# A transposed product in two matmuls instead of three: streaming encoder trunk on one Trainium2 core

## The chip, the cores and the metric

The kernel runs as one launch on one core of a Trainium2 chip. Its time is device time in microseconds. Beside the timed runs there is one profiled execution, whose trace gives each instruction's start and duration on each engine: TensorE (PE, with its weight loads as PEld), VectorE (DVE), ScalarE (ACT), GpSimd (POOL) and SyncE (SP, which only issues DMAs here).

## What is computed

The input x is 256 tokens by 1024 channels, float32. Two layers of three sub-layers each follow one another: FFN, mixer, FFN. Mixer 0 is an S5 state-space block, mixer 1 is gMLP. So the order is FFN, S5, FFN, FFN, gMLP, FFN.

```python
def _swiglu(x, w_in, w_out):                 # D_MODEL 1024, D_FF 2816
    gate, up = jnp.split(x @ w_in, 2, axis=-1)
    return (jax.nn.silu(gate) * up) @ w_out
# FFN sub-layer:   h = layernorm(sqrt(2)*h + 0.5*swiglu(h))
# gMLP sub-layer:  z = gelu(h @ w_in + b_in); u, v = split(z); v = layernorm(v)
#                  s = masked W_s applied over the tokens of a 128-block, per head; h = layernorm(sqrt(2)*h + (u*s) @ w_out)
```

## The kernel before

**Numbers in two parts.** Each float32 operand of a large product is split into hi (rounded to fp32r, TensorE's format here) and lo, the rest. A product takes three matmuls: hi by hi, hi by lo, lo by hi. Weights are split on the chip: `Stream` (lines 42 to 151) loads blocks of 128 x 2048 (1 MB) in a fixed order on SP's queue into three raw buffers, ScalarE casts raw to hi, VectorE subtracts hi from raw to give lo. At most five blocks are split ahead (`N_SPLIT`). Each call of `ws.tick()` splits one more block if a place is free; with `ws.lazy` set (in the FFN chunks) the lo subtraction is issued one tick after its hi.

**Tokens.** `make_xt` transposes the 256 tokens (two parts t of 128) on TensorE and writes them to `xt` as hi (`xth`) and lo (`xtl`), for eight slices k of 128 channels. In memory `xt` is ordered part, hi or lo, k, token, so for one k and hi the two token parts lie apart.

**An FFN** has 11 chunks of 256 hidden columns, gate and up. The first two are computed with tokens as the stationary operand and weights as the moving one (`step_in`, `mm3`, 512 columns). From chunk 2 on (from chunk 1 in the first FFN), `chunk_in` computes them transposed: weights (128 x 128) stationary, tokens moving, 256 columns, through `mm3t` (line 205). A chunk has four groups (m, g): m the half of 128 hidden columns, g = 0 gate and g = 1 up. A group is 8 slices k of three matmuls. Gate and up of one m share a PSUM bank. When both are done, `act_t` does Silu of the gate out of PSUM on ScalarE (line 397), and VectorE multiplies the up half in PSUM by it (line 398). `split_gt`, after the next group, splits the result into hi and lo for the output product (lines 406, 407). After chunk c come two output steps for chunk c - 2 (`step_out`, 12 matmuls of 512 columns each). The last three chunks' output products come in `close`, together with the residual, the LayerNorm, and the transposes of the next sub-layer's tokens.

**u of gMLP.** `step_u` computes one head of u (128 columns) transposed, like a group above: 24 matmuls through `mm3t`, then Gelu out of PSUM on ScalarE (line 558), then a tick. For heads 4 to 7, `spatial` follows at once: four matmuls into a PSUM tile `sps` and, for two heads, two VectorE operations each (lines 580, 581); then `split_g` splits the gated result (lines 587, 588).

**What sets the order.** The kernel is written under a manual schedule: each engine runs its instructions in the order in which the program issues them, first in, first out, and waits only on semaphores for data and for buffers. The pools rotate their buffers. All PSUM tiles that matter here (`ips`, `tps`, `zps`, `sps`) come from one pool of four banks (`mm_p`), in turn; the output sums have four banks of their own.

In S5, `yx` (line 1122) uses the same `xt` storage for its own operand of the gate product.

Of the kernel before, what the change touches and what calls it, by code (L numbers as in the profile page):

```python
# [9 lines left out]
F32 = mybir.dt.float32  # L10
F32R = mybir.dt.float32r
I32 = mybir.dt.int32
AF = mybir.ActivationFunctionType
ALU = mybir.AluOpType
PSUM = bass.MemoryType.PSUM

P = 128
D = 1024
KD = D // P
SEQ = 256  # L20
DFF = 2816
FC = 256
NCH = DFF // FC
# [131 lines left out]
def hybrid(ctx: ExitStack, tc: tile.TileContext, a: dict, out: bass.AP, subs=SUBS):  # L155
    nc = tc.nc
# [4 lines left out]
    xt_p = pool("xt", 1)  # L161
    g_p = pool("g", 2)
# [3 lines left out]
    mm_p = pool("mm", 4, space=PSUM)  # L166
# [7 lines left out]
    nc.gpsimd.memset(mhalf, -0.5)  # L174

    h = [const.tile([P, D], F32, name=f"h{t}") for t in range(2)]
    xt = xt_p.tile([P, 2, 2, KD, P], F32R, name="xt")
    xth, xtl = ([xt[:, t, j] for t in range(2)] for j in range(2))

    ws = Stream(nc, raw_p, split_p)  # L180

# [22 lines left out]

    def mm3t(ps, wh, wl, k, start, stop):

        xh, xl = (xt[:, :, j, k] for j in range(2))
        nc.tensor.matmul(ps, wh, xh, start=start, stop=False)  # L208
        nc.tensor.matmul(ps, wh, xl, start=False, stop=False)  # L209
        nc.tensor.matmul(ps, wl, xh, start=False, stop=stop)  # L210

    def load_ln(li, si, eng):
        g = ln_p.tile([P, D], F32, tag="gam", name="gam")
        b = ln_p.tile([P, D], F32, tag="bet", name="bet")
        eng.dma_start(out=g, in_=a["ln_g"][li, si:si + 1, :].broadcast_to([P, D]))
        eng.dma_start(out=b, in_=a["ln_b"][li, si:si + 1, :].broadcast_to([P, D]))
        return g, b
# [51 lines left out]
    def done(ids):  # L269
        for i in ids:  # L270
            ws.done(i)
# [61 lines left out]
    def ffn(ids, li, si, first, last):  # L333
# [4 lines left out]
        def new_gt(c, m):  # L338
            if (c, m) not in gts:
                gts[c, m] = gt_p.tile([P, 2, SEQ], F32R, tag="gt", name="gt")  # L340
            return gts[c, m]
# [31 lines left out]
        def chunk_in(c):  # L373

            for m in range(2):
                ps = mm_p.tile([P, 2, SEQ], F32, tag="mm", name="ips")
                for g in range(2):
                    for k in range(KD):
                        wh, wl = ws.get(ids["in"][c][k // 4])
                        s = slice(512 * (k % 4) + FC * g + P * m, 512 * (k % 4) + FC * g + P * m + P)  # L380
                        mm3t(ps[:, g], wh[:, s], wl[:, s], k, k == 0, k == KD - 1)
                    if (m, g) == (1, 1):
                        done(ids["in"][c])
                    split_gt()
                    if g:
                        act_t(c, m, ps)
                    if (m, g) == (0, 1):
                        finish_g()
                    if (m, g) == (1, 1) and c == NCH - 1:
                        split_gt()  # L390
                    ws.tick()

        def act_t(c, m, ps):
            sgg = g_p.tile([P, 2, SEQ], F32, tag="sgg", name="sgg")
            sg, g = sgg[:, 0], sgg[:, 1]
            x = new_gt(c, m)
            nc.scalar.activation(sg, ps[:, 0], AF.Silu)  # L397
            nc.vector.tensor_tensor(g, ps[:, 1], sg, op=ALU.mult)  # L398
            later.append((x, g))

        later = []

        def split_gt():
            while later:
                x, g = later.pop()
                nc.scalar.copy(x[:, 0], g)  # L406
                nc.vector.tensor_tensor(x[:, 1], g, x[:, 0].bitcast(F32), op=ALU.subtract)  # L407
# [59 lines left out]
            step_in(1, 1)  # L467
        ws.lazy = True
        for c in range(2, NCH):
            chunk_in(c)  # L470
            if c == NCH - 1:
                gb = load_ln(li, si, nc.gpsimd)
            if c < NCH - 1:
                step_out(c - 2, 0)
                step_out(c - 2, 1)
# [53 lines left out]
    def gmlp(plan, par, pool, li, si, first, last):  # L529
        cols, rows = plan  # L530
        b_v, vg, vb, b_u, b_s, _, w_st = par
        v = [pool.tile([P, D], F32, name=f"v{t}") for t in range(2)]
        u = [pool.tile([P, SEQ], F32, name=f"u{h}") for h in range(HEADS)]
# [16 lines left out]
        def step_u(hd):  # L550

            ids = cols[2 + hd // 4]
            ps = mm_p.tile([P, SEQ], F32, tag="mm", name="zps")
            for k in range(KD):
                wh, wl = ws.get(ids[k // 4])
                s = slice(512 * (k % 4) + P * (hd % 4), 512 * (k % 4) + P * (hd % 4) + P)
                mm3t(ps, wh[:, s], wl[:, s], k, k == 0, k == KD - 1)
            nc.scalar.activation(u[hd], ps, AF.Gelu_apprx_tanh, bias=b_u[:, hd:hd + 1])
            if hd % 4 == 3:
                done(ids)  # L560
            ws.tick()
# [38 lines left out]
        for hd in range(HEADS):  # L600
            step_u(hd)
            if hd >= 4:
                spatial(2 * hd - 8)
                for x in range(2):
                    split_g(2 * hd - 8 + x)
# [408 lines left out]
    def s5(plan, res, qp, li, si, first, last):  # L1014
# [105 lines left out]
            nc.scalar.copy(yx(ct, 0), yc.rearrange("p (t k) -> p t k", t=2))  # L1120

        def yx(ct, j):
            return xt[:, :, j, ct]

        def split_y(ct):
            yc = y[ct // 4][:, ct % 4]
# [50 lines left out]
        later = []  # L1177
# [96 lines left out]
    with tc.manual_schedule():  # L1274
# [9 lines left out]
        for n in range(2):  # L1284
            s = slice(512 * n, 512 * n + 512)
# [7 lines left out]
        for n, (kind, li, si) in enumerate(subs):  # L1293
            first, last = n == 0, n == len(subs) - 1
# [49 lines left out]
```

## Time and profile before

| | us |
|---|---|
| timed runs | 986.35, 982.47, 985.27 (median 985.27) |
| profiled execution | 983.81 |
| its span, first to last instruction | 981.7 |
| TensorE busy | 948.4 (97%), 6988 matmuls |
| VectorE busy | 650.1 (66%) |
| ScalarE busy | 425.9 (43%) |
| moved from HBM | 184.07 MB, 198 GB/s with the writes over the span |

Matmuls are pipelined and their durations overlap, so the pace of TensorE is read from start to start. The granted clock is a share of full speed: 1.00 is 2.4 GHz, 0.50 is 1.2 GHz. In a row, `out<-in` names the tiles and "<-" behind an idle time names what ended it. Line numbers are those of the kernel before.

### The profile page before, as it was taken

The numbers are of one execution on the slowest core, as the hardware profiler recorded it, in microseconds if no ns is written. First come the engines' busy times: TensorE is split into PE (matmuls) and PEld (weight loads), VectorE is DVE, ScalarE is ACT, GpSimd is POOL, SyncE is SP. The second block draws the span as 40 slices with busy tenths as digits, with TensorE's granted clock in tenths as the row PEclk, the third lists the DMA queues.
The fourth block names the chain that finished last, engine by engine and source line by source line (L and its number), as shares of the span: only waits on it lengthen the run. The fifth ranks groups of instructions, "written<-read, shape, count | busy, mean of one in ns | idle before, by whom it ended". The sixth has DMA issues, their size and how long they took to land.

```text
span 981.7 us, 16616 instructions
## 1 busy us (share of the span) xinstructions
PE 948.4 (97%) x6988; PEld 860.6 (88%) x6988; DVE 650.1 (66%) x801; ACT 425.9 (43%) x504; POOL 165.6 (17%) x249
## 2 busy tenths in 40 slices
PE   7997999999999999999999999999999999999996
PEld 5996989978887789999997999999879879999995
DVE  5858999778797955455467644536588766453635
ACT  5554355644335445343423634344345445433430
POOL 1868811001572100000002000000011010000001
PEclk9998999999899999999999999999999999999998
DMA  8874796968645665746466674655447457555521
GB/s 278 224 223 162 265 280 220 289 214 285 221 146 183 189 209 179 237 133 233 152 200 216 211 272 154 204 182 179 164 155 275 129 173 265 163 194 192 168 90 43
DMA packets 133354, 195.10 MB, mean 199 GB/s; under 512 B 7120, under 2 KB 103936, under 8 KB 133280
## 3 DMA queue, kind: packets, MB, share of 16 engines
q1 hardware_dynamic: 128432, 182.34, 56.0%
q0 software_dynamic: 4560, 11.19, 3.9%
q8 instruction: 54, 0.88, 0.4%
q10 hardware_dynamic: 288, 0.52, 0.1%
q14 instruction: 20, 0.16, 0.0%
HBM read 184.07 MB, written 9.96 MB: 198 GB/s over the span
## 4 chain that ended last, share of the span: by engine, by line
PE 66%; DVE 18%; DMA 6%; POOL 3%; issue 3%; ACT 2%; SPq 0%; POOLq 0%; DVEq 0%; ACTq 0%
PE ips L210 11%; PE ips L209 11%; PE ips L208 11%; PE acc L201 7%; PE acc L202 7%; PE acc L203 7%; DVE lo L89 4%; DVE lo L97 4%; PE pps L1075 2%; DVE pq L639 1%; PE ips L203 1%; DMA raw<-in_ffn_w_out 1%; DVE prod L639 1%; ACT hi L96 1%; PE ips L201 1%
## 5 line engine op out<-in xcount | busy, mean ns | idle before, releaser
L210 PE MATMUL ips<-xt,lo 128*128 128x256 f32 x1184 | 335.5, 283 | 2.8 <-DVE lo L89 2.2
L208 PE MATMUL ips<-xt,hi 128*128 128x256 f32 x1184 | 335.4, 283 | 0.0
L209 PE MATMUL ips<-xt,hi 128*128 128x256 f32 x1184 | 335.0, 283 | 0.0
L89 DVE TENSOR_TENSOR lo<-raw,hi 128x2048 fp32r<-128x2048 f32 x107 | 242.9, 2292 | 11.1 <-ACT hi L88 10.7
L210 PEld LDWEIGHTS ips<-xt,lo 128*128 128x128 f32 x1184 | 227.1, 192 | 3.6 <-DVE lo L89 2.8
L208 PEld LDWEIGHTS ips<-xt,hi 128*128 128x128 f32 x1184 | 227.1, 192 | 1.5
L209 PEld LDWEIGHTS ips<-xt,hi 128*128 128x128 f32 x1184 | 227.1, 192 | 1.4
L88 ACT CAST hi<-raw 128x2048 fp32r<-128x2048 f32 x107 | 204.1, 1909 | 47.2 <-PE acc L203 26.6
L202 PE MATMUL acc<-lo,gt 128*128 128x512 f32 x352 | 138.5, 393 | 6.6 <-DVE lo L89 6.6
L398 DVE TENSOR_TENSOR sgg<-ips,sgg 128x256 f32<-128x256 f32 x74 | 31.3, 423 | 163.9 <-ACT sgg L397 163.8
L201 PE MATMUL acc<-hi,gt 128*128 128x512 f32 x352 | 138.7, 394 | 0.6 <-ACT gt L406 0.5
L203 PE MATMUL acc<-hi,gt 128*128 128x512 f32 x352 | 137.8, 391 | 0.0
L397 ACT ACTIVATE sgg<-ips 128x256 f32<-128x256 f32 x74 | 28.3, 383 | 214.2 <-PE ips L210 213.0
L221 POOL TENSOR_SCALAR rstd<-mv 128x1 f32<-128x1 f32 x14 | 10.4, 741 | 636.8 <-DVE mv L247 613.0
L97 DVE TENSOR_TENSOR lo<-raw,hi 128x2048 fp32r<-128x2048 f32 (+2 forms) x52 | 89.6, 1754 | 22.6 <-ACT hi L96 22.4
L202 PEld LDWEIGHTS acc<-lo,gt 128*128 128x128 f32 x352 | 66.7, 189 | 20.0 <-DVE lo L89 7.5
L201 PEld LDWEIGHTS acc<-hi,gt 128*128 128x128 f32 x352 | 66.7, 189 | 14.2 <-ACT gt L406 1.3
L203 PEld LDWEIGHTS acc<-hi,gt 128*128 128x128 f32 x352 | 66.5, 189 | 14.3 <-DVE gt L407 0.3
L96 ACT CAST hi<-raw 128x2048 fp32r<-128x2048 f32 (+2 forms) x52 | 74.5, 1482 | 3.6 <-DMA raw<-in_ffn_w_in 2.9
L407 DVE TENSOR_TENSOR gt<-sgg,gt 128x256 fp32r<-128x256 f32 x74 | 31.3, 423 | 59.5 <-ACT gt L406 59.5
L406 ACT CAST gt<-sgg 128x256 fp32r<-128x256 f32 x74 | 30.1, 406 | 68.1 <-DVE sgg L398 67.9
L201 PE MATMUL ips<-hi,xt 128*128 128x512 f32 x112 | 44.9, 401 | 3.8 <-ACT xt L192 2.3
(230 smaller groups left out, 1227.0 us busy)
## 6 DMA issues: line engine op xcount, KB each, us to landing
raw<-in_ffn_w_in SPq DMA_DIRECT2D x172, 512.0 KB, 5.8
raw<-in_ffn_w_out SPq DMA_DIRECT2D x44, 1024.0 KB, 5.2
raw<-in_g_w_in SPq DMA_DIRECT2D x8, 1024.0 KB, 5.8
rows<-w SPq DMA_DIRECT2D x8, 512.0 KB, 3.8
raw<-in_s_w_in SPq DMA_DIRECT2D x4, 1024.0 KB, 7.2
raw<-in_s_w_glu SPq DMA_DIRECT2D x4, 1024.0 KB, 5.2
w<-rows SPq DMA_DIRECT2D x8, 512.0 KB, 5.3
tc<-tc SPq DMA_DIRECT2D x16, 256.0 KB, 5.4
```

The costliest lines, as they stand in the source:

```text
L88: nc.scalar.copy(hi, raw)
L89: self.unfinished.append(lambda: nc.vector.tensor_tensor(lo, raw, hi.bitcast(F32), op=ALU.subtract))
L96: nc.scalar.copy(hi[:, s], raw[:, s])
L97: eng[p % len(eng)].tensor_tensor(lo[:, s], raw[:, s], hi[:, s].bitcast(F32), op=ALU.subtract)
L201: nc.tensor.matmul(ps, xh, wh, start=start, stop=False)
L202: nc.tensor.matmul(ps, xh, wl, start=False, stop=False)
L203: nc.tensor.matmul(ps, xl, wh, start=False, stop=stop)
L208: nc.tensor.matmul(ps, wh, xh, start=start, stop=False)
L209: nc.tensor.matmul(ps, wh, xl, start=False, stop=False)
L210: nc.tensor.matmul(ps, wl, xh, start=False, stop=stop)
L398: nc.vector.tensor_tensor(g, ps[:, 1], sg, op=ALU.mult)
L407: nc.vector.tensor_tensor(x[:, 1], g, x[:, 0].bitcast(F32), op=ALU.subtract)
```

## The change

For one k, `xt` now holds hi of part 0, hi of part 1, lo of part 0, lo of part 1 side by side. A new `mm2t` replaces the three matmuls by two: the weights' hi meets all four pieces in one matmul of 512 columns, whose result has two halves in one PSUM bank; the weights' lo then meets the tokens' hi (256 columns), added to the first half. The two halves have to be added afterwards: ScalarE copies the second half to SBUF, and VectorE adds the first half out of PSUM. A new `chunk_in2` does this for each group of a chunk, with a bank for each group, and with Silu and the product now on SBUF; it is used by the three FFNs after the first. `step_u` does the same before its Gelu. The first FFN keeps `chunk_in` and `mm3t`, on the new layout.

```diff
@@ -174,8 +174,8 @@
     nc.gpsimd.memset(mhalf, -0.5)
 
     h = [const.tile([P, D], F32, name=f"h{t}") for t in range(2)]
-    xt = xt_p.tile([P, 2, 2, KD, P], F32R, name="xt")
-    xth, xtl = ([xt[:, t, j] for t in range(2)] for j in range(2))
+    xt = xt_p.tile([P, KD, 2, 2, P], F32R, name="xt")
+    xth, xtl = ([xt[:, :, j, t] for t in range(2)] for j in range(2))
 
     ws = Stream(nc, raw_p, split_p)
 
@@ -204,10 +204,16 @@
 
     def mm3t(ps, wh, wl, k, start, stop):
 
-        xh, xl = (xt[:, :, j, k] for j in range(2))
+        xh, xl = (xt[:, k, j].rearrange("p t c -> p (t c)") for j in range(2))
         nc.tensor.matmul(ps, wh, xh, start=start, stop=False)
         nc.tensor.matmul(ps, wh, xl, start=False, stop=False)
         nc.tensor.matmul(ps, wl, xh, start=False, stop=stop)
+
+    def mm2t(ps, wh, wl, k):
+
+
+        nc.tensor.matmul(ps.rearrange("p j n -> p (j n)"), wh, xt[:, k].rearrange("p j t c -> p (j t c)"), start=k == 0, stop=False)
+        nc.tensor.matmul(ps[:, 0], wl, xt[:, k, 0].rearrange("p t c -> p (t c)"), start=False, stop=k == KD - 1)
 
     def load_ln(li, si, eng):
         g = ln_p.tile([P, D], F32, tag="gam", name="gam")
@@ -384,6 +390,32 @@
                     split_gt()
                     if g:
                         act_t(c, m, ps)
+                    if (m, g) == (0, 1):
+                        finish_g()
+                    if (m, g) == (1, 1) and c == NCH - 1:
+                        split_gt()
+                    ws.tick()
+
+        def chunk_in2(c):
+
+            for m in range(2):
+                sgg = g_p.tile([P, 2, SEQ], F32, tag="sgg", name="sgg")
+                for g in range(2):
+                    ps = mm_p.tile([P, 2, SEQ], F32, tag="mm", name="ips")
+                    for k in range(KD):
+                        wh, wl = ws.get(ids["in"][c][k // 4])
+                        s = slice(512 * (k % 4) + FC * g + P * m, 512 * (k % 4) + FC * g + P * m + P)
+                        mm2t(ps, wh[:, s], wl[:, s], k)
+                    if (m, g) == (1, 1):
+                        done(ids["in"][c])
+                    split_gt()
+                    nc.scalar.copy(sgg[:, g], ps[:, 1])
+                    nc.vector.tensor_tensor(sgg[:, g], sgg[:, g], ps[:, 0], op=ALU.add)
+                    if g == 0:
+                        nc.scalar.activation(sgg[:, 0], sgg[:, 0], AF.Silu)
+                    else:
+                        nc.vector.tensor_tensor(sgg[:, 1], sgg[:, 1], sgg[:, 0], op=ALU.mult)
+                        later.append((new_gt(c, m), sgg[:, 1]))
                     if (m, g) == (0, 1):
                         finish_g()
                     if (m, g) == (1, 1) and c == NCH - 1:
@@ -467,7 +499,7 @@
             step_in(1, 1)
         ws.lazy = True
         for c in range(2, NCH):
-            chunk_in(c)
+            (chunk_in if first else chunk_in2)(c)
             if c == NCH - 1:
                 gb = load_ln(li, si, nc.gpsimd)
             if c < NCH - 1:
@@ -550,12 +582,14 @@
         def step_u(hd):
 
             ids = cols[2 + hd // 4]
-            ps = mm_p.tile([P, SEQ], F32, tag="mm", name="zps")
+            ps = mm_p.tile([P, 2, SEQ], F32, tag="mm", name="zps")
             for k in range(KD):
                 wh, wl = ws.get(ids[k // 4])
                 s = slice(512 * (k % 4) + P * (hd % 4), 512 * (k % 4) + P * (hd % 4) + P)
-                mm3t(ps, wh[:, s], wl[:, s], k, k == 0, k == KD - 1)
-            nc.scalar.activation(u[hd], ps, AF.Gelu_apprx_tanh, bias=b_u[:, hd:hd + 1])
+                mm2t(ps, wh[:, s], wl[:, s], k)
+            nc.scalar.copy(u[hd], ps[:, 1])
+            nc.vector.tensor_tensor(u[hd], u[hd], ps[:, 0], op=ALU.add)
+            nc.scalar.activation(u[hd], u[hd], AF.Gelu_apprx_tanh, bias=b_u[:, hd:hd + 1])
             if hd % 4 == 3:
                 done(ids)
             ws.tick()
@@ -1120,7 +1154,7 @@
             nc.scalar.copy(yx(ct, 0), yc.rearrange("p (t k) -> p t k", t=2))
 
         def yx(ct, j):
-            return xt[:, :, j, ct]
+            return xt[:, ct, j]
 
         def split_y(ct):
             yc = y[ct // 4][:, ct % 4]
```

## Rows read from the trace of the kernel before

**Rows 1.** The page: busy time of each engine; the chain that ended last, by line.
```profile
PE 948.4 (97%) x6988; PEld 860.6 (88%) x6988; DVE 650.1 (66%) x801; ACT 425.9 (43%) x504; POOL 165.6 (17%) x249
...
PE ips L210 11%; PE ips L209 11%; PE ips L208 11%; PE acc L201 7%; PE acc L202 7%; PE acc L203 7%; DVE lo L89 4%; DVE lo L97 4%; PE pps L1075 2%; DVE pq L639 1%; PE ips L203 1%; DMA raw<-in_ffn_w_out 1%; DVE prod L639 1%; ACT hi L96 1%; PE ips L201 1%
```

**Rows 2.** Table by stretches: length, engines' busy time (count), clock, DMA; an FFN, u.
```profile
343.40:517.40 174.00, 173.86 (x1175) 161.25 (x1176) 92.25 (x89) 70.88 (x76) 1.69 (x2) 1.00 0.57 192
...
735.20:761.60 26.40, 26.40 (x224) 26.40 (x223) 22.68 (x31) 14.03 (x20) 2.77 (x4) 1.00 0.76 272
```

**Rows 3.** Waits of TensorE from 343 us on: total us, times, longest.
```profile
PE ips L201 <- ACT xt L192: 2.3, 3, 0.8
PE zps L201 <- DVE xt L193: 1.0, 1, 1.0
```

**Rows 4.** Timeline of TensorE: start us, duration us, engine, line, operation.
```profile
372.75 0.28 PE L208 MATMUL ips<-xt,hi 128*128 128x256 f32 x1
...
384.26 0.40 PE L201 MATMUL acc<-hi,gt 128*128 128x512 f32 x1
...
503.00 0.28 PE L210 MATMUL ips<-xt,lo 128*128 128x256 f32 x1
503.12 0.40 PE L201 MATMUL acc<-hi,gt 128*128 128x512 f32 x1
503.35 0.40 PE L202 MATMUL acc<-lo,gt 128*128 128x512 f32 x1
...
517.43 0.27 PE L187 MATMUL tps<-ident,h 128*128 128x128 f32 x1
```

**Rows 5.** Table by stretches, of line 208 alone: one FFN.
```profile
343.00:533.00 190.00, 81.53 (x288) 55.25 (x288) 1.00 0.57 191
```

**Rows 6.** The page's groups: count, busy us, mean ns; idle before, and why.
```profile
L398 DVE TENSOR_TENSOR sgg<-ips,sgg 128x256 f32<-128x256 f32 x74 | 31.3, 423 | 163.9 <-ACT sgg L397 163.8
...
L397 ACT ACTIVATE sgg<-ips 128x256 f32<-128x256 f32 x74 | 28.3, 383 | 214.2 <-PE ips L210 213.0
```

**Rows 7.** Timeline of VectorE: the LayerNorm of an FFN's first token part.
```profile
515.79 1.42 DVE L231 SCALAR_TENSOR_TENSOR h<-r,rstd,bet 128x512 f32<-128x512 f32 x2 [0.46 <-POOL rstd L222]
```

**Rows 8.** Line 193 alone: min, median, max ns, first and last start.
```profile
L193 DVE TENSOR_TENSOR xt<-tps,xt x24: 673/681/692, 5.3 to 798.0; 128x512 fp32r<-128x512 f32 x24
```

**Rows 9.** Groups of the u stage, 735.2 to 761.6 us.
```profile
L97 DVE TENSOR_TENSOR lo<-raw,hi 128x2048 fp32r<-128x2048 f32 x5 | 11.4, 2289 | 3.9 <-ACT hi L96 3.9
L96 ACT CAST hi<-raw 128x2048 fp32r<-128x2048 f32 x5 | 9.4, 1899 | 0.0
...
L558 ACT ACTIVATE u<-zps,b_u 128x256 f32<-128x256 f32 x8 | 3.6, 470 | 2.7 <-PE zps L210 2.7
```

**Rows 10.** Timeline of ScalarE: Gelu of head 0.
```profile
741.78 0.46 ACT L558 ACTIVATE u<-zps,b_u 128x256 f32<-128x256 f32 x1
```

**Rows 11.** Timeline of VectorE from u to the LayerNorm of gMLP.
```profile
746.07 2.28 DVE L97 TENSOR_TENSOR lo<-raw,hi 128x2048 fp32r<-128x2048 f32 x1
...
754.27 0.42 DVE L580 TENSOR_TENSOR x<-sps,b_s 128x256 f32<-128x256 f32 x1
...
768.14 0.42 DVE L588 TENSOR_TENSOR gated<-u,gated 128x256 fp32r<-128x256 f32 x1 [0.19 <-ACT gated L587]
...
779.24 1.41 DVE L231 SCALAR_TENSOR_TENSOR h<-r,rstd,bet 128x512 f32<-128x512 f32 x2 [0.46 <-POOL rstd L222]
```

**Rows 12.** Timeline of TensorE: the transposes of the next sub-layer's tokens.
```profile
781.50 0.60 PE L187 MATMUL tps<-ident,h 128*128 128x128 f32 x4
```

**Rows 13.** Table by stretches, as rows 2, around TensorE's longest idle time.
```profile
82.00:84.00 2.00, 0.83 (x4) 0.32 (x3) 2.00 (x4) 1.95 (x4) 1.50 (x7) 1.00 0.00 0
84.00:86.00 2.00, 0.00 (x0) 0.00 (x0) 1.97 (x5) 2.00 (x2) 1.83 (x4) 0.89 0.62 243
86.00:88.00 2.00, 0.00 (x0) 0.00 (x0) 2.00 (x3) 1.98 (x2) 1.84 (x3) 0.50 0.05 19
...
92.00:94.00 2.00, 2.00 (x10) 1.59 (x9) 2.00 (x2) 0.00 (x0) 2.00 (x2) 0.90 0.95 337
```

## The prediction

> **What bounds the kernel now.** I read the page first: TensorE is busy for 97% of the span, and the chain that ended last has the three matmul lines of the transposed product (208 to 210, 11% of the span each) and the three of the plain one (201 to 203, 7% each) as its largest items [rows 1]. A busy TensorE is not yet a full one, so I went to the stages. The table by stretches shows the first of the three FFNs that the change touches (174.0 us, from its second xt to the last matmul ahead of the next; the other two look alike) and the u stage of gMLP (26.4 us). In both TensorE is busy all the way at full clock; VectorE is busy for 92 of 174 us and ScalarE for 71, but in the u stage VectorE for 22.68 of 26.4 [rows 2]. The list of TensorE's waits, from 343 us to the end, holds four in all, 3.3 us, each for the xt copies at a sub-layer's start [rows 3]. So in those stretches TensorE's own rhythm sets the time, and that rhythm is read from start to start: 96 matmuls of 256 columns run from 372.75 to 384.26 us, 119.9 ns each; 63 of 512 columns run from 503.12 to 517.43 us, 227.1 ns each [rows 4]. Twice the columns cost 107.2 ns more, so each matmul has 12.7 ns that don't grow with its width. (The 283 and 390 ns of the duration column overlap with the next matmul and are no pace.)
>
> **What goes.** A triplet of three 256-wide matmuls (359.7 ns) becomes one of 512 and one of 256. The same 768 columns pass; one matmul and one weight load go. From the pace of rows: 227.1 + 119.9 = 347.0 ns, 12.7 ns less. No row shows the two widths in alternation, nor xt as a 512-wide moving operand. The ends are 3 x 107.2 = 321.6 ns (no fixed part left) and 359.7 ns (nothing gained). I take 347.0, because where a 256 meets a 512 in the trace, at 503.00, 503.12, 503.35, each keeps its own pace [rows 4]. Count: 9 chunks x 4 groups x 8 steps = 288 triplets per FFN, and line 208 stands 288 times in such an FFN [rows 5]; three FFNs make 864, and u has 8 heads x 8 steps = 64. Gain: 864 x 12.7 ns = 10.97 us in the FFNs, 64 x 12.7 = 0.81 us in u.
>
> The Trainium skill, TensorE: Matmul & The Clock Gate, section Back-to-back issue gap, gives an isolated warm gap of N/2.4 + 2.5 ns, a fixed part of 2.5 ns where the rows show 12.7. By it the whole saving would be 928 x 2.5 = 2.3 us. The rows disagree at both widths (its gaps are 109 and 216 ns), so the sum goes by the rows.
>
> **What is added in the FFNs.** Each of the 36 groups of an FFN now needs a ScalarE copy of one half of PSUM and a VectorE add of the other, and Silu and the product come behind them. The nearest rows are 383 ns (Silu from PSUM) to 470 ns (Gelu from PSUM, with a bias) for the copy, and 423 ns for the product out of PSUM [rows 6, 9]; I take 0.39, by the row of plain shape, and 0.42 us. A chunk with its two output steps takes 96 x 119.9 + 24 x 227.1 ns = 17.0 us; four copies and adds put 1.6 us on ScalarE and 1.7 us on VectorE, which had 41% and 53% of it [rows 2]. The danger is order, since both engines work first in, first out: copy, add (behind a lo subtraction of 2.29 us, if one runs), Silu (waits for the add), and the next hi cast behind it. What TensorE needs of this in time is the PSUM bank. The ring has four banks and a group takes one, so a bank is due again after three more groups and two output steps, 3 x 2.78 + 5.45 = 13.8 us; copy and add, even behind a hi (1.90) and two lo (4.6) [rows 9], are through in under 8 us. The weights are split a chunk ahead. The worst place is chunk 2, with VectorE still behind from step_in: walked in program order, the last split that chunk 3 needs ends at 368.3 us, 2.5 later than before, and is due at 373.6. At the last chunk the chain copy, add, product, hi, lo is 0.45 us longer than Silu, product, hi, lo, and hi and lo of its second half are due 3.4 us after the chunk's end, in step 3 of close; ready at about 2.5. It also pushes the hi/lo splits and the LayerNorm of close by 0.45 us; its first half ended at 516.5 us with the transposes that read it at 517.43, so it fits [rows 4, 7]. Cost: nothing, hidden under TensorE; if that cover went, one add plus copy per group, 0.8 us x 108.
>
> The xt layout puts the four pieces of one k side by side. Writers now store four runs of 128 instead of one of 512. Line 193 already writes both straight and in the strided order of S5, all 24 within 673 to 692 ns [rows 8]. I cost it at nothing; ends 0 and a doubled 0.68 us in the few writes near a wait, under 1 us.
>
> **What is added in u: the term that decides.** Here VectorE has no slack, and ScalarE must now wait for it in the middle of each head: copy, add on VectorE, Gelu, and behind Gelu the hi cast of the next weight block, whose lo then sits before the next add. I walked the two queues in program order with the durations of the rows [rows 6, 9]; the same walk without copies and adds puts each ScalarE and VectorE instruction of the u stage of before within 0.1 us of its row.
> VectorE is through with norm_v(1) at 746.07 us, where before the first lo began [rows 11]. The copy of head 0 is done long before; its add takes 746.07 to 746.5, Gelu 746.6 (before 741.78 [rows 10]), the hi behind it 746.9 to 748.8, lo 748.9 to 751.1. Add 1 waits behind that lo: ends 751.5. Heads 2 and 3 follow at 1.3 us each: adds end 752.8 and 754.1. Then Gelu 3, hi 754.5, lo 756.5 to 758.7; add 4 ends 759.1; Gelu 4, hi 759.5, lo 761.5 to 763.7; the first gate operations of line 580 at 763.7 (before 754.27), 9.4 us late; each of the next three heads adds some 0.3 to 1.0 to that, by its own add between the gate operations, and the last gated lo stands at 779.2 (before 768.14), 11.0 us late [rows 11].
> TensorE needs the ring of four banks: u0 u1 u2 u3 u4 s0 u5 s1 u6 s2 u7 s3 (s: the gate products). Before, a u bank was free with its Gelu. Now: u4 waits for add 0, 0.34 us; s0, ready at 749.36, for add 1, 2.24; u5 for add 2, 0.50; u6 for add 4, 2.74; s2 for the line 580 reads of s0, 3.03; u7 for add 5, 0.94; later in close_mixer gated 6, 0.15. Sum 9.94 us.
> In close the LayerNorm is 11.0 us late and TensorE 9.94 - 0.81 = 9.1; the first half of h was ready at 780.0 us [rows 11] for transposes at 781.50 [rows 12], 1.4 us of slack with 0.1 for the signal, so 11.0 - 9.1 - 1.4 = 0.5 us is waited there.
> Bounds of this term: 0 if adds and copies were to slip into VectorE's gaps (3.9 us of them lie ahead of the lo subtractions, all waits for ScalarE's hi [rows 9]), and 9.94 + 0.5 + 8 x (0.47 - 0.39) = 11.1 us if a copy costs what a Gelu does. I take 9.94 + 0.5, since the walk meets the rows of before.
>
> **The sum**, against the profiled execution, 983.81 us (span 981.7 and 2.1 around it): -10.97 - 0.81 + 9.94 + 0.5 = -1.34 us, 982.5 us. The median of the three runs shown is 985.27, 1.46 above the profiled one, so the forecast in its terms is 985.27 - 1.34 = 983.9 us.
>
> **Rivals.**
> Clock falls in u: the waits of 2.74 and 3.03 us leave TensorE idle. In the one long idle stretch of the trace it stopped at 82.8 us, and the granted clock, 0.89 over 84 to 86 and then 0.50 (1.2 GHz), fell some 2.7 us after; it was back at about 92.4, 6.8 us at half rate [rows 13]. For: the same length of gap. Against: matmuls stand between the gaps. A spell costs up to 3.4 us; much of it lies beside the two queues, I take 2.5: 986.4, with two spells up to 990.7.
> The waits of u don't come: the adds run ahead of the lo subtractions and TensorE keeps its pace as in the FFNs. For: VectorE has gaps in sum. Against: program order on both queues, and 22.68 us busy of 26.4 before 3.4 us of adds. Then 985.27 - 10.97 - 0.81 = 973.5, faster.
> Slower: the fixed part doesn't go with the instruction. The 512-wide matmul on xt behind a 256-wide one would take 2 x 119.9 ns, the pair 359.7. For: all 512-wide rows have weights as moving operand and stand among their own kind. Against: 227.1 ns over 63 of them. The gain is 0, the waits of u stay: 985.27 + 9.94 + 0.5 = 995.7. The sign turns at a pair of 348.4 ns, where 928 savings pay for 10.4 us. By the fixed part of 2.5 ns in the Trainium skill, TensorE: Matmul & The Clock Gate, Back-to-back issue gap, it would be 993.4; the trace, with its 12.7, does not bear that out.
>
> **Chances.** Forecast 0.58 (983.9, its own range 981 to 988, from the copy's and the pair's price); clock 0.18; no waits in u 0.15; no gain 0.09. The range of 974 to 991 takes in the sum's own bounds, one or two clock spells and the nearer half of the faster case; it leaves out the other half, the slower case and a tail, some 0.19. A measurement of this kernel tells 0.5%, 4.9 us, from no change. Faster than 980.3: 0.15 and a tail of 0.04, 0.19. Slower than 990.2: 0.09 and 0.05 from two spells, 0.14. Same: 0.67.
>
> **What would show it.** 928 matmuls and weight loads fewer (6988 to 6060). Start to start 227 and 120 ns in alternation; a pair above 348 refutes the gain. The three FFN stretches each 3.7 us shorter and without a TensorE wait. The u stage from 26.4 to about 35.5 us, with TensorE waiting on VectorE's new add, longest 3.0 us, and on line 580's reads; Gelu of head 0 some 4.8 us later than before against the stage's start. The forecast is wrong if u keeps 26 us, if an FFN stretch shows waits per chunk, or if the granted clock leaves 1.00 in u.

## The result: 990.4 us, 0.5% slower than before

The changed kernel took 990.43 us (median of 6 runs, 986.35 to 991.07), the kernel before 984.71 us on the same chip (6 runs, 982.47 to 986.35). The ratio is 1.0053, with a 95% interval of 1.0035 to 1.0070. The forecast was 983.9 us in a range of 974 to 991: the time lies inside the range, but the kernel became slower by 5.7 us where the forecast had 1.3 us less.

The page of the changed kernel answers to [rows 1]: 928 matmuls and 928 weight loads are gone, as counted, and VectorE and ScalarE have 116 more instructions each. Yet TensorE's busy time did not fall (948.4 us before).

```profile
PE 950.2 (96%) x6060; PEld 815.8 (83%) x6060; DVE 696.0 (70%) x917; ACT 469.8 (48%) x620; POOL 169.6 (17%) x249
```

To see where the time went I cut both traces at the same work: a stretch begins with the transposes of a sub-layer's second token part and ends with the first transposes of the next sub-layer. That is one table by stretches for each kernel: window, length, then busy us (count) of PE, PEld, DVE, ACT, POOL, then TensorE's granted clock, the DMA's busy share and GB/s. First before (FFN 1, FFN 2, gMLP), then after.

```profile
341.60:517.43 175.83, 174.94 (x1184) 162.09 (x1183) 94.08 (x91) 72.34 (x79) 1.69 (x2) 1.00 0.57 192
531.43:708.13 176.70, 175.79 (x1193) 162.91 (x1192) 94.09 (x91) 73.41 (x81) 3.22 (x5) 1.00 0.62 205
722.14:781.50 59.36, 58.40 (x369) 52.76 (x368) 49.43 (x65) 27.60 (x32) 6.15 (x8) 1.00 0.62 213
```

```profile
343.83:517.88 174.05, 173.15 (x896) 146.65 (x895) 107.85 (x126) 85.97 (x115) 1.69 (x2) 1.00 0.58 194
531.92:706.91 174.99, 174.11 (x904) 147.51 (x903) 107.98 (x126) 86.81 (x117) 3.21 (x5) 1.00 0.62 208
720.92:790.27 69.35, 62.13 (x304) 51.88 (x303) 51.46 (x71) 30.63 (x40) 6.14 (x8) 0.95 0.54 182
```

The FFNs are 1.78 and 1.71 us shorter (the third 1.78), where the prediction's 10.97 us were 3.66 for each. The gMLP is 9.99 us longer, where the prediction had -0.81 + 9.94 + 0.5 = 9.63. The stretch ahead of the first FFN, which the change touches only through the layout, ended at 343.83 instead of 341.60; that lies within the scatter (the kernels below have the same code ahead of it, and their starts lie between 340.37 and 345.92; the layout alone gave 341.06). So the u stage came as forecast, and half of the gain that was to pay for it is missing.

The timeline of the changed kernel's TensorE at the start and the end of a chunk, which answers to [rows 4], shows the missing half. Columns: start us, duration us.

```profile
391.48 0.39 PE L215 MATMUL ips<-xt,hi 128*128 128x512 f32 x1
...
402.07 0.40 PE L215 MATMUL ips<-xt,hi 128*128 128x512 f32 x1
402.31 0.28 PE L216 MATMUL ips<-xt,lo 128*128 128x256 f32 x1
402.42 0.40 PE L215 MATMUL ips<-xt,hi 128*128 128x512 f32 x1
402.66 0.28 PE L216 MATMUL ips<-xt,lo 128*128 128x256 f32 x1
402.77 0.40 PE L201 MATMUL acc<-hi,gt 128*128 128x512 f32 x1
403.01 0.40 PE L202 MATMUL acc<-lo,gt 128*128 128x512 f32 x1
403.25 0.40 PE L203 MATMUL acc<-hi,gt 128*128 128x512 f32 x1
403.49 0.40 PE L201 MATMUL acc<-hi,gt 128*128 128x512 f32 x1
```

Read from start to start, with rows in steps of 10 ns: a 512-wide matmul takes some 240 ns here and not 227, a 256-wide one some 110, and the chunk's 32 pairs (391.48 to 402.77) take 352.8 each. Even the first three 512-wide ones of the other product behind the chunk (402.77 to 403.49) take some 240 each. From the stretches, which hold these output steps too, a pair costs 359.7 - 1780 / 288 = 353.5 ns; the prediction took 347.0. No wait stands there: the list of TensorE's waits has none in the FFNs but the xt copies of [rows 3], and it has the new ones in u.

```profile
PE sps L610 <- DVE x L614: 2.8, 1, 2.8
PE ips L201 <- ACT xt L192: 2.3, 3, 0.8
PE sps L610 <- DVE u L591: 2.0, 1, 2.0
PE zps L215 <- DVE u L591: 1.4, 2, 0.9
PE zps L201 <- DVE xt L193: 1.0, 1, 1.0
```

### The profile page after: what moved, and what is told of

It reads as the page before. It is cut to its first block, busy times and chain, and to the rows that moved or that the text cites. A ratio compares the mean times of both kernels' runs of the same rounds, so it can differ in the third digit from the quotient of the medians.

```text
span 988.7 us, 15015 instructions
## 1 busy us (share of the span) xinstructions
PE 950.2 (96%) x6060; PEld 815.8 (83%) x6060; DVE 696.0 (70%) x917; ACT 469.8 (48%) x620; POOL 169.6 (17%) x249
## 4 chain that ended last, share of the span: by engine, by line
PE 63%; DVE 19%; DMA 6%; issue 4%; POOL 3%; ACT 3%; SPq 0%; POOLq 0%; DVEq 0%; ACTq 0%
PE ips L215 20%; PE ips L216 10%; PE acc L201 7%; PE acc L203 7%; PE acc L202 7%; DVE lo L97 4%; DVE lo L89 4%; ACT hi L96 2%; PE pps L1109 2%; DMA raw<-in_ffn_w_out 1%; DVE pq L673 1%; PE ips L203 1%; DMA bq<-in_s_b_re 1%; DVE prod L673 1%; PE ips L201 1%
## 5 line engine op out<-in xcount | busy, mean ns | idle before, releaser
L215 PE MATMUL ips<-xt,hi 128*128 128x512 f32 x864 | 306.3, 398 | 0.0
L215 PEld LDWEIGHTS ips<-xt,hi 128*128 128x128 f32 x864 | 162.3, 188 | 39.8
L216 PEld LDWEIGHTS ips<-xt,lo 128*128 128x128 f32 x864 | 163.2, 189 | 1.1
L413 DVE TENSOR_TENSOR sgg<-sgg,ips 128x256 f32<-128x256 f32 x108 | 45.5, 421 | 124.7 <-ACT sgg L412 124.5
L412 ACT COPY sgg<-ips 128x256 f32<-128x256 f32 x108 | 40.1, 372 | 116.3 <-PE ips L216 116.3
L208 PE MATMUL ips<-xt,hi 128*128 128x256 f32 x320 | 90.8, 284 | 0.0
L209 PE MATMUL ips<-xt,hi 128*128 128x256 f32 x320 | 90.5, 283 | 0.0
```

What stands on the lines that cost most here:

```text
L215: nc.tensor.matmul(ps.rearrange("p j n -> p (j n)"), wh, xt[:, k].rearrange("p j t c -> p (j t c)"), start=k == 0, stop=False)
L216: nc.tensor.matmul(ps[:, 0], wl, xt[:, k, 0].rearrange("p t c -> p (t c)"), start=False, stop=k == KD - 1)
```

## The experiments

"Wide" is a matmul of 512 columns, "narrow" one of 256. FFN 1 and FFN 2 are the two stretches of the tables above (before: 175.83 and 176.70 us). Theory C was that each change between the widths costs; its rivals are named with each run. The first four kernels ran together, then e5 to e8, then the last four (by the numbers of their labels); the kernel before ran with each set and took 984.42, 984.81 and 983.27 us. From the second heading on, the edits are against the first kernel (FFNs of the change, u as before) where nothing else is said.

**The change's two parts apart, and the layout alone**

The first kernel has the FFNs of the change and u as before; the third has only the layout; the fourth only u. Against the changed kernel:

```diff
 # FFNs only, and layout only: u as before
-            ps = mm_p.tile([P, 2, SEQ], F32, tag="mm", name="zps")
+            ps = mm_p.tile([P, SEQ], F32, tag="mm", name="zps")
...
-                mm2t(ps, wh[:, s], wl[:, s], k)
-            nc.scalar.copy(u[hd], ps[:, 1])
-            nc.vector.tensor_tensor(u[hd], u[hd], ps[:, 0], op=ALU.add)
-            nc.scalar.activation(u[hd], u[hd], AF.Gelu_apprx_tanh, bias=b_u[:, hd:hd + 1])
+                mm3t(ps, wh[:, s], wl[:, s], k, k == 0, k == KD - 1)
+            nc.scalar.activation(u[hd], ps, AF.Gelu_apprx_tanh, bias=b_u[:, hd:hd + 1])
 # u only, and layout only: FFNs as before
-            (chunk_in if first else chunk_in2)(c)
+            chunk_in(c)
```

> Two matmuls in the three FFNs alone; u of gMLP goes back to three matmuls and Gelu out of PSUM. My theory, that u costs 10.0 us of waits and the FFNs give back only 1.8 us each because a pair of matmuls takes 353.5 ns and not 347: gMLP's stretch between its transposes back at 59.4 us, each FFN stretch 1.8 us under before, in all 984.7 - 5.3 = 979.4 us. Rival, that the new order of xt slows the first FFN and S5 (the changed kernel reached its second FFN 2.2 us later than before): 981.6 us. Rival, that the waits of u are not the cause of gMLP's loss: it stays at 69 us, 989 us.

Measured: 979.55 us, ratio 0.9954 (0.9936 to 0.9972). FFN 1, FFN 2 and gMLP:

```profile
344.93:518.97 174.04, 173.17 (x897) 146.64 (x896) 107.82 (x126) 85.97 (x115) 1.69 (x2) 1.00 0.58 194
532.98:707.92 174.94, 174.04 (x904) 147.46 (x903) 107.99 (x126) 86.84 (x117) 3.22 (x5) 1.00 0.63 208
721.96:781.32 59.36, 58.40 (x369) 52.76 (x368) 49.43 (x65) 27.59 (x32) 6.14 (x8) 1.00 0.64 213
```

The FFNs alone make the kernel faster, by half of what was forecast; gMLP is that of before.

> Only the new order of xt; all products with three matmuls as before. My theory: no change, 984.7 us, the 2.2 us by which the changed kernel reached its second FFN later are chance of that run. Rival (layout costs): first FFN and S5 together 2.2 us longer in every run, 986.9 us.

Measured: 984.64 us, ratio 1.0007 (0.9991 to 1.0023); FFN 1 is 175.83 us and gMLP 59.36, both those of before to the hundredth. The layout costs nothing that shows, within some 0.2% of the whole.

> Two matmuls in u of gMLP alone, the FFNs with three as before. My theory: gMLP's stretch 10.0 us longer, the rest as before, 994.7 us, TensorE waiting on the new add and on line 580's reads by some 9 us. Rival (the loss of gMLP comes from the FFN ahead of it, through late splits): gMLP as before, 984 us.

Measured: 992.36 us, ratio 1.0094 (1.0072 to 1.0115). FFN 1 takes 175.78 us, as before, and the gMLP:

```profile
723.80:793.01 69.21, 61.91 (x304) 51.83 (x303) 51.31 (x71) 30.63 (x40) 6.14 (x8) 0.95 0.53 182
```

The gMLP's 9.85 us come from u alone. The two parts add up: 0.9954 and 1.0094 make 1.0048, the change has 1.0053.

**The same pairs in another order**

> As e1, but a group runs its eight 512-wide matmuls first and its eight 256-wide ones after them, so the two widths change over once in eight. Theory C (the changeover between widths costs the 6.5 ns per pair): 512 at 227 ns and 256 at 120 ns, pair 347.0, each FFN 3.7 us under before, 984.7 - 11.0 = 973.7 us. Theory O (the 512-wide token operand, or the write of a whole bank, costs it): pair stays at 353.5, as e1, 979.4 us.

The edit, on the first kernel; mm_hi and mm_lo are the wide and the narrow matmul of mm2t apart:

```diff
-                    for k in range(KD):
-                        wh, wl = ws.get(ids["in"][c][k // 4])
-                        s = slice(512 * (k % 4) + FC * g + P * m, 512 * (k % 4) + FC * g + P * m + P)
-                        mm2t(ps, wh[:, s], wl[:, s], k)
+                    for k0 in range(0, KD, 8):
+                        for part in range(2):
+                            for k in range(k0, k0 + 8):
+                                w = ws.get(ids["in"][c][k // 4])[part]
+                                s = slice(512 * (k % 4) + FC * g + P * m, 512 * (k % 4) + FC * g + P * m + P)
+                                (mm_hi, mm_lo)[part](ps, w[:, s], k)
```

Measured: 974.46 us, ratio 0.9905 (0.9886 to 0.9924); the FFNs are 172.56 and 173.48 us, 3.27 and 3.22 less than before. The same instructions, only their order changed, give back most of the missing gain: 5.1 us over the first kernel. So the wide token operand and the whole bank don't cost by themselves (theory O), and the price lies in the order of the two widths. The timeline of a chunk (equal matmuls in a row are merged):

```profile
389.93 1.98 PE L219 MATMUL ips<-xt,hi 128*128 128x512 f32 x8
391.75 1.11 PE L222 MATMUL ips<-xt,lo 128*128 128x256 f32 x8
392.70 2.00 PE L219 MATMUL ips<-xt,hi 128*128 128x512 f32 x8
394.54 1.11 PE L222 MATMUL ips<-xt,lo 128*128 128x256 f32 x8
...
401.08 0.40 PE L201 MATMUL acc<-hi,gt 128*128 128x512 f32 x1
```

Eight wide ones behind other wide ones take 1.82 us (389.93 to 391.75), behind narrow ones 1.84 (392.70 to 394.54). In the trace's starts to the ns the second run takes 27 ns more, all in its first five matmuls (233, 236, 229, 232, 231, and from then on 227): the price is not paid at the change alone.

> The three FFNs in two matmuls, u as before, the matmuls of a group in the order wide, wide, narrow, narrow instead of wide, narrow: half as many changes of width as in the first experiment, same columns, same operands. Theory C (each change of width costs, about 6.5 ns for a pair that goes there and back): a pair of matmuls takes (353.0 + 347.0) / 2 = 350.0 ns, so each FFN of 288 triplets is 288 x (359.7 - 350.0) = 2.8 us shorter than before, three of them 8.4 us, near 976. Rival O (the wide token operand or the whole bank written costs by itself, and the run of eight gained for another reason, such as the same operand kind eight times in a row): no proportion between changes and cost; the time stays at the first experiment's 979.6 or is already the 974.5 of runs of eight.

The edit: `range(0, KD, 8)` and `k0 + 8` above become 2. Measured: 973.03 us, ratio 0.9894 (0.9861 to 0.9928), the FFNs 172.28 and 173.17 us, 3.55 and 3.53 shorter than before. FFN 1:

```profile
340.37:512.65 172.28, 171.40 (x896) 145.98 (x895) 107.76 (x126) 85.99 (x115) 1.69 (x2) 1.00 0.59 196
```

Both expectations missed. Theory C, a price for each change of width, wanted half of the loss to stay; nearly all of it went (3.54 of the sum's 3.66 us), with four times as many changes as in runs of eight. This run's timeline of TensorE has a chunk's 32 pairs from 404.29 to 415.43, so 348 ns for a pair, 1 above the forecast's 347.0.

```profile
404.29 0.61 PE L219 MATMUL ips<-xt,hi 128*128 128x512 f32 x2
404.75 0.40 PE L222 MATMUL ips<-xt,lo 128*128 128x256 f32 x2
404.98 0.63 PE L219 MATMUL ips<-xt,hi 128*128 128x512 f32 x2
...
415.43 0.40 PE L201 MATMUL acc<-hi,gt 128*128 128x512 f32 x1
```

**What it is not**

> The three FFNs with three matmuls of 256 columns as before, but hi x hi written to one half of a bank and hi x lo to the other, and the copy and add of the two halves behind each group as in the change; u as before. If the copies and adds of 108 groups lie wholly beside TensorE and the tile of a whole bank is no cost, every stage is as before: FFN stretches within 0.2 us of 175.8, 176.7 and 177.6, total within 1 us of before. Rival: the longer release of the bank (copy .37 and add .42 us where one Gelu of about .6 stood) or the order of ScalarE's work holds TensorE back: each 0.1 us of wait per group of a stage gives 3.6 us for each FFN, so anything over 2 us longer in all speaks for it, and then part of the FFNs' missing gain in the change is not TensorE's pace.

```diff
-        nc.tensor.matmul(ps.rearrange("p j n -> p (j n)"), wh, xt[:, k].rearrange("p j t c -> p (j t c)"), start=k == 0, stop=False)
+        for j in range(2):
+            nc.tensor.matmul(ps[:, j], wh, xt[:, k, j].rearrange("p t c -> p (t c)"), start=k == 0 and j == 0, stop=False)
```

Measured: 985.09 us, ratio 1.0008 (0.9988 to 1.0028), the FFNs 175.77 and 176.73 us, as before within 0.06. All 108 copies and adds stand in them, and cost nothing; nor does writing the two halves of one bank in turn.

> The three FFNs with two matmuls of 512 columns for each weight block, high weights and low weights in turn, both against both token parts (so low x low is added, work that the change does not have); u as before. It alternates between high and low weights as the change does and writes a whole bank each time, with no change of width. Theory C (the change of width is what costs): each matmul .2267 us as elsewhere in the kernel, a pair .4535, each FFN 288 x (453.5 - 359.7) ns = 27.0 us longer than before, three of them 81 us, total near 1065.5. Rival W (going from high to low weights, or writing the other parts of a bank, costs the 6.5 ns per pair): a pair .460, each FFN 28.9 us longer, total near 1071.

```diff
-        nc.tensor.matmul(ps[:, 0], wl, xt[:, k, 0].rearrange("p t c -> p (t c)"), start=False, stop=k == KD - 1)
+        nc.tensor.matmul(ps.rearrange("p j n -> p (j n)"), wl, xt[:, k].rearrange("p j t c -> p (j t c)"), start=False, stop=k == KD - 1)
```

Measured: 1065.34 us, ratio 1.0833 (1.0774 to 1.0891, two runs), the FFNs 26.68 and 26.80 us longer than before. By that a matmul takes (359.7 + 26740 / 288) / 2 = 226 ns, and the timeline has some 230 for each:

```profile
412.03 0.39 PE L216 MATMUL ips<-xt,lo 128*128 128x512 f32 x1
412.26 0.39 PE L215 MATMUL ips<-xt,hi 128*128 128x512 f32 x1
412.49 0.39 PE L216 MATMUL ips<-xt,lo 128*128 128x512 f32 x1
```

High and low weights in turn, and the same token block read twice in a row, cost nothing while the width stays the same.

> FFNs in two matmuls, wide and narrow one by one in turn as in the change, but the narrow one is never of the same token operand as its neighbours (wide 0, narrow 2, wide 1, narrow 3, wide 2, narrow 0, wide 3, narrow 1, and so on); u as before. The runs of two differed from the first experiment in two things, half as many changes of width and no narrow matmul directly beside the wide one of its own token block. Theory N (the neighbour: reading the same token block again at once costs the 6.5 ns): the cost goes, pair .347, each FFN stretch 3.5 us shorter than before, total near 973. Theory S (a single matmul between two of the other width costs, whatever it reads): pair .3535 as in the change, each stretch 1.8 us shorter, total near 979.5.

```diff
-                    for k in range(KD):
-                        wh, wl = ws.get(ids["in"][c][k // 4])
+                    for part, k in [(part, k) for i in range(KD) for part, k in ((0, i), (1, i // 4 * 4 + (i + 2) % 4))]:
+                        w = ws.get(ids["in"][c][k // 4])[part]
...
-                        mm2t(ps, wh[:, s], wl[:, s], k)
+                        (mm_hi, mm_lo)[part](ps, w[:, s], k)
```

Measured: 979.49 us, ratio 0.9966 (0.9943 to 0.9989), the FFNs 173.98 and 174.99 us: 1.85 and 1.71 less than before, as with the change's own order. The neighbour's operand is not it. (In this edit and the next the stop flag moves with the last matmul of a group.)

> FFNs in two matmuls in runs of two, each first narrow directly behind the wide one of its own token block (wide 0, narrow 0, narrow 1, wide 1, wide 2, narrow 2, narrow 3, wide 3, and so on); u as before. With the run before it this makes a table of two by two: single or in twos, same or other neighbour. Theory N: every wide one stands beside the narrow one of its block, so the pair is .3535, each FFN stretch 1.8 us shorter than before, total near 979.5. Theory S: pair .347 to .348, each stretch 3.5 us shorter, total near 973.

```diff
-                    for part, k in [(part, k) for i in range(KD) for part, k in ((0, i), (1, i // 4 * 4 + (i + 2) % 4))]:
+                    for part, k in [x for k in range(0, KD, 2) for x in ((0, k), (1, k), (1, k + 1), (0, k + 1))]:
```

The edit is against the run before it. Measured: 972.69 us, ratio 0.9891 (0.9839 to 0.9942, two runs), the FFNs 172.29 and 173.16 us, the same as the other order in twos within 0.01. The table of two by two is clear: one by one loses about 1.9 us per FFN against the sum with either neighbour, in twos 0.1 with either.

> FFNs in two matmuls in runs of four wide, four narrow; u as before. Theory S: no single one, so like runs of two (stretches 3.5 us shorter than before) or eight (3.3 us), total 973 to 974.5. A cost for each narrow run's end in proportion to its changes would have made twos dearer than eights, which they weren't (3.5 against 3.3 us gained); if fours gain under 3.0 us, the cost has no simple dependence on the length of a run.

The edit is that of the runs of eight, with 4 in its place. Measured: 976.01 us, ratio 0.9930 (0.9909 to 0.9950), the FFNs 173.11 and 174.10 us. A chunk's 32 pairs:

```profile
390.74 1.07 PE L219 MATMUL ips<-xt,hi 128*128 128x512 f32 x4
...
401.94 0.40 PE L201 MATMUL acc<-hi,gt 128*128 128x512 f32 x1
```

The gain is 2.72 and 2.60 us, under the 3.0 that the expectation set as its bound. So theory S, that only a single one costs, doesn't hold as it was put either. What is missing of 3.66 us per FFN, over 288 pairs, and over the returns from narrow to wide, the one at a group's end counted; then, from starts alone, a pair within a chunk and the 24 wide matmuls of the output steps behind it (359.7 ns for a triplet and 5.47 us before):

| order | gain per FFN, us | missing per pair, ns | returns per 8 pairs | missing per return, ns | pair in a chunk, ns | output steps, us |
|---|---|---|---|---|---|---|
| one by one | 1.78 | 6.5 | 8 | 6.5 | 352.8 | 5.50 |
| in twos | 3.54 | 0.4 | 4 | 0.8 | 348.0 | 5.45 |
| in fours | 2.66 | 3.5 | 2 | 14 | 350.0 | 5.49 |
| in eights | 3.25 | 1.4 | 1 | 11 | 348.3 | 5.47 |

(The gain is the mean of FFN 1 and FFN 2, one by one in the first kernel; 3.66 less the gain, times 1000, over 288, is the third column, and that times 8 over the returns the fifth. The last two columns are read in FFN 1's whole chunks, which agree within 0.1 ns and 0.01 us.) Within a chunk twos and eights are alike, 1.0 and 1.3 ns over 347.0; part of the lead of the twos lies in the output steps behind. In neither reading does the loss follow the number of returns.

> FFNs in two matmuls in the order of the change, wide, narrow, wide, narrow, but low x high is added into the other half of the bank (onto high x low; the sum of the halves is the same), so that a wide matmul never begins on the columns that the narrow one before it has just written; u as before. Theory B (the next wide matmul waits on the half that was just written): pair .347, each FFN stretch 3.5 us shorter than before, total near 973. Theory S or N: no difference from the first experiment, pair .3535, each stretch 1.8 us shorter, total near 979.5.

```diff
-        nc.tensor.matmul(ps[:, 0], wl, xt[:, k, 0].rearrange("p t c -> p (t c)"), start=False, stop=k == KD - 1)
+        nc.tensor.matmul(ps[:, 1], wl, xt[:, k, 0].rearrange("p t c -> p (t c)"), start=False, stop=k == KD - 1)
```

Measured: 978.34 us, ratio 0.9948 (0.9920 to 0.9976), the FFNs 174.02 and 174.96 us, as with the change's order. Theory B falls: the half that was just written is not waited for.

**u with the Gelu one head behind**

> The FFNs in two matmuls with the wide ones of a group first (second experiment, 974.46), and u in two matmuls as in the change, but the Gelu of head h is issued behind the copy of head h+1, so that ScalarE no longer stands at a Gelu that waits for VectorE's add; the last head's Gelu stands directly behind its add. Theory Q (the 10 us of u are ScalarE's and VectorE's queues waiting on each other: Gelu for the add, the next split for the Gelu, the next add behind the split's subtraction): by a walk through the two queues the first matmul of the closing projection is some 2 us later than before and the gMLP takes 59.4 + 2.0 to 2.5, near 61.6, so the total is near 976.7. Rival L (the 10 us are the added work itself: eight copies of .35 and eight adds of .42 us on engines that are full there, 6.2 us, and TensorE's wait for banks): the gMLP stays at 66 to 69 and the total at 981 to 984.5. Rival F (TensorE's clock, which fell twice in this stage): a clock that still falls to .5 would leave the stage long with the waits gone.

The edit, against the changed kernel's u; the FFNs are those of the runs of eight:

```diff
             nc.scalar.copy(u[hd], ps[:, 1])
-            nc.vector.tensor_tensor(u[hd], u[hd], ps[:, 0], op=ALU.add)
-            nc.scalar.activation(u[hd], u[hd], AF.Gelu_apprx_tanh, bias=b_u[:, hd:hd + 1])
+            for x in ([hd - 1] if hd else []) + ([hd] if hd == 7 else []):
+                if x == hd:
+                    nc.vector.tensor_tensor(u[hd], u[hd], ps[:, 0], op=ALU.add)
+                nc.scalar.activation(u[x], u[x], AF.Gelu_apprx_tanh, bias=b_u[:, x:x + 1])
+            if hd < 7:
+                nc.vector.tensor_tensor(u[hd], u[hd], ps[:, 0], op=ALU.add)
```

Measured: 976.78 us, ratio 0.9916 (0.9891 to 0.9942). The gMLP, and ScalarE at its start:

```profile
716.81:778.98 62.17, 59.01 (x304) 49.32 (x303) 50.76 (x71) 30.15 (x40) 6.14 (x8) 1.00 0.60 203
```

```profile
736.46 0.35 ACT L598 COPY u<-zps 128x256 f32<-128x256 f32 x1
736.72 1.92 ACT L96 CAST hi<-raw 128x2048 fp32r<-128x2048 f32 x1
...
741.20 0.51 ACT L602 ACTIVATE u<-u,b_u 128x256 f32<-128x256 f32 x1 [2.30 <-DVE u L604]
```

The same copies, adds and Gelus stand in it, and the gMLP is 2.8 us longer than before instead of 9.9: theory Q. The hi cast starts right behind the first copy, where in the changed kernel it stood behind a Gelu that waited 4.39 us for VectorE:

```profile
745.31 0.51 ACT L592 ACTIVATE u<-u,b_u 128x256 f32<-128x256 f32 x1 [4.39 <-DVE u L591]
745.73 1.89 ACT L96 CAST hi<-raw 128x2048 fp32r<-128x2048 f32 x1
```

TensorE's waits on u are down from 6.2 us to 1.4 and the granted clock stays at 1.00. So the added work itself costs little (rival L falls), and rival F is no cause of its own, since the clock's fall went with the waits. The walk had 2.0 to 2.5 us. TensorE's waits hold 0.7 us for VectorE's h at the end of the gMLP; what is over the walk was not followed up.

## Why the prediction was wrong, point by point

**The term that failed** is "From the pace of rows: 227.1 + 119.9 = 347.0 ns, 12.7 ns less." For wide and narrow matmuls in turn it is 353.5 ns, 6.2 ns less than a triplet. That makes 1.78 us per FFN and 5.3 us over all three instead of 10.97, and turns the sign: put into the prediction's own sum, -928 x 6.2 ns + 9.94 + 0.5 = +4.7 us, 990.0 us; 990.43 were measured. It also agrees with the point that the prediction gave for the turn, a pair of 348.4 ns. That 990.4 lies inside the range is luck: the room above the forecast, up to 990.7, was made for spells of a slow clock, not for this.

The reason given for 347.0, that each width keeps its own pace where a 256 meets a 512, rested on two steps of 10 ns resolution at one seam. Another seam of the same trace of before shows what was missed: from 401.24 on, six 512-wide matmuls behind the narrow ones take 1.38 us, 230 ns each, some 20 ns more in all than six times 227.1 (the rows between are left out).

```profile
401.12 0.28 PE L210 MATMUL ips<-xt,lo 128*128 128x256 f32 x1
401.24 0.40 PE L201 MATMUL acc<-hi,gt 128*128 128x512 f32 x1
...
402.62 0.39 PE L201 MATMUL acc<-hi,gt 128*128 128x512 f32 x1
```

The kernel before has such seams only where a group is followed by an output step; the change put one into every pair. The mechanism of the gain was right: in twos 3.54 us of each 3.66 came, so nearly all of the part that doesn't grow with the width goes with the instruction. The Trainium skill, TensorE: Matmul & The Clock Gate, section Back-to-back issue gap, has a fixed part of 2.5 ns, by which an estimate is 288 x 2.5 ns = 0.7 us per FFN. The runs in twos gained five times that, and the measurement decides.

**What it is that costs**: shown is that the order of the widths sets it, by the same instructions in six orders, and that it is not the operand's neighbour, the half written, the whole bank, the alternation of high and low weights, the copies and adds, or the layout. Not shown is why ones cost most and fours more than twos and eights; each theory that gave a price by count fell. Not tested is the weight load that goes with each matmul, 188 ns on the page of the changed kernel, longer than the some 120 from a narrow matmul's start to the next: every order has the same loads, and no run is without them. So the cause behind the order stays open.

**Hidden in the FFNs**: right. No wait of TensorE, and the FFNs with copies and adds but without the wide matmul are those of before. Their sizes were 372 ns (0.39 taken) and 421 ns (0.42).

**The layout**: right, nothing that shows.

**u**: right to 0.4 us in all, and for the reason given, the two queues; the split between waits and clock was another (below). Against the stretch's start, Gelu of head 0 comes 4.75 us later than before (4.8 forecast), the first gate operation 9.3 (9.4), the last gated lo 10.9 (11.0), the normalized first part of h 10.9. This is VectorE in the changed kernel; the add of head 1 stands behind a lo (747.65), and the first gate operation behind three of them, as in the walk:

```profile
744.86 0.42 DVE L591 TENSOR_TENSOR u<-u,zps 128x256 f32<-128x256 f32 x1
747.65 2.29 DVE L97 TENSOR_TENSOR lo<-raw,hi 128x2048 fp32r<-128x2048 f32 x1 [2.38 <-ACT hi L96]
749.86 0.41 DVE L591 TENSOR_TENSOR u<-u,zps 128x256 f32<-128x256 f32 x1
...
760.14 2.29 DVE L97 TENSOR_TENSOR lo<-raw,hi 128x2048 fp32r<-128x2048 f32 x1 [2.37 <-ACT hi L96]
762.36 0.42 DVE L614 TENSOR_TENSOR x<-sps,b_s 128x256 f32<-128x256 f32 x1
...
788.94 1.42 DVE L237 SCALAR_TENSOR_TENSOR h<-r,rstd,bet 128x512 f32<-128x512 f32 x2 [0.46 <-POOL rstd L228]
```

**The clock rival** came true and cost little. The granted clock fell to 0.50 twice in u, after the waits of 2.0 and 2.8 us; columns as in the tables by stretches:

```profile
750.00:752.00 2.00, 1.58 (x9) 1.41 (x10) 0.70 (x2) 1.20 (x4) 0.00 (x0) 0.82 0.47 78
752.00:754.00 2.00, 2.00 (x7) 1.71 (x7) 0.42 (x1) 1.51 (x4) 0.00 (x0) 0.50 0.95 387
...
764.00:766.00 2.00, 1.48 (x10) 1.19 (x9) 1.78 (x6) 1.19 (x3) 0.00 (x0) 0.73 0.99 292
766.00:768.00 2.00, 2.00 (x8) 1.71 (x7) 1.77 (x6) 1.08 (x3) 0.00 (x0) 0.50 0.57 200
```

The prediction priced two spells at 5 us or more. All of gMLP was only 0.36 us over the sum without them: the two queues were as late as the walk had them, slow matmuls took the place of waits, which came to 6.2 us instead of 9.94, and the 0.5 us of waiting for h in close did not come. No run parts the waits from the clock, so this price is worked out and not measured by itself. The chance of 0.18 also left out what the trace of before shows beside "the one long idle stretch": a second spell in S5, with a clock of 0.85 over 248 to 250 us and 0.50 over 250 to 256, where the longest idle time just ahead was 1.75 us.

**No gain at all**, the slower rival, was nearest in sign and place: a wide matmul on xt behind a narrow one was where the gain failed. Its size, all of the gain, was twice too much, and its mechanism (the fixed part stays) is refuted by the runs in twos.

**The version that beats both** is the FFNs in two matmuls, in twos, with u as before: 973.03 us, ratio 0.9894 (0.9861 to 0.9928). Some of that lies ahead of the FFNs, in a stretch that varies by some us from run to run; the three FFNs alone give about 3 x 3.54 = 10.6 us.

## What to carry to other kernels

A pace read from long rows of one width held here for that width alone; before a sum mixes two, add up several starts behind each seam in the trace, and if instructions of two widths must alternate, try them in twos, since order alone was worth 1.8 us per FFN here. Where two engines work first in, first out, an operation that waits for the other engine holds up all that stands behind it: the same copies, adds and Gelus cost 9.9 us in one order and 2.8 in another. A fall of the clock beside queues that are late anyway is to be priced by what then waits for TensorE: here some 0.4 us where 5 or more were priced.

## What the runs showed of the hardware that was not expected

- Matmuls of 512 and 256 columns one by one in turn took 352.8 ns a pair within a chunk, in twos 348.0, at a granted clock of 1.00 in both. The slowing lasts: in runs of eight the first five wide ones behind narrow ones took 228 to 236 ns each, where 227 is the pace.
- The loss is not in proportion to the changes of width: by the stretches, per return from narrow to wide, 6.5 ns one by one, 0.8 in twos, 14 in fours, 11 in eights.
- The granted clock fell to 0.50 after idle stretches of 2.04 and 2.81 us between matmuls in u; with TensorE's waits there at 0.6 us or less it stayed at 1.00.
